# Tying a decode step's key products to the prompt's attention steps, and reordering the memory norm at the start

## The chip, the cores and the metric

One core of a Trainium2 chip runs the whole kernel. The metric is the device time of one execution in microseconds (us). A change of about 0.2% (4 us) is what a measurement of this kernel can tell from none.

## The reference

One layer of a decoder trunk is computed in fp32 for a prompt of 1024 tokens and for 8 decode rows with 2048 cached tokens each:

```python
xn = RMSNorm(x);  q, k, v, B, C, h, xq = split(xn @ w_in)
# branch A: stick-breaking attention, 8 heads x 64
z = q.k / 8 + b_sb[head]
log_keep = where(mask, log_sigmoid(-z), 0)
after = reverse_cumsum(log_keep) - log_keep
y_sb = where(mask, exp(log_sigmoid(z) + after), 0) @ v
# branch B: y_conv = B * causal_conv3(C * h)
# branch M: 4 heads, softmax attention into 256 memory tokens
mk, mv = split(RMSNorm(mem) @ w_mem_kv)
# merge by sigmoid gates of xn @ w_gate, project by w_o, add; then the squared-relu FFN, add
```

The decode rows take their past keys and values from pages of a pool (16 pages of 128 tokens for each row) and their memory keys from a cache. The outputs are also the new keys, values, conv states and the memory's keys and values.

## The kernel before

Every fp32 operand of a large matmul is split into a high part (a cast to fp32r on ScalarE) and a low part (the difference), and each product is three matmuls: high by high, high by low, low by high (`mm3`, L141 to L143). A weight block of 128 x 1024 comes by one DMA of 512 KB into one of two raw buffers (`weights`, L133); `split` casts it (L119) and subtracts (L120). The raw buffer is free for the next block when the subtraction is done. The subtraction runs on VectorE, but for the eight blocks of the memory's keys and values (`mk0` to `mk3`, `mv00` to `mv14`), whose blocks are given to GpSimd.

TensorE's order is written out by hand. A small planner (`Stream`) keeps a clock of its own: it walks a list of units (GEMMs of 10.3 us by its cost for the 1032 tokens), and between matmuls fires events that other generators asked for at a time of that clock: strips of the prompt's attention (`attention`), the memory attention (`xattn`), the decode rows (`decode`), and small transposes. TensorE executes in just this order. The order of the other engines and of the DMA queue is decided when the program is built, by a list scheduler with a timing model: it takes whatever is ready, the higher priority first. On the chip each engine then runs its own list strictly in order.

The parts that matter here:

- The start. The rows of the memory are loaded, squared and summed on ScalarE (L299), scaled (L300), put through Ln and Exp (L301, L302) and a Newton step (`newton`, L150 to L153), and multiplied (L305). TensorE transposes them (L314), ScalarE and VectorE make their high and low parts (L318, L319), and the memory's eight units begin. The prompt's rows go the same way, their transposes put between the memory's matmuls.
- The prompt's attention. A strip is 128 queries of two heads against up to eight key blocks; strips of five and more blocks are cut in two halves. Each head and half is one call of `zhalf`: four ScalarE steps, then on VectorE L639, L641, a scan (L642) and L648, with Ln and Exp on ScalarE. Eight strips make a pair of heads with 24 calls of `zhalf`, that is 96 of these VectorE steps; there are four pairs. The planner gives a pair 138.4 us (`ATT_NS`).
- The decode keys. For each row, eight tiles of two key pages (512 KB) come by DMA on SP (L835) into three buffers; VectorE multiplies a tile by the query (L928) and sums over each head (L929). With eight tiles of memory keys that is 72 such pairs of instructions ("products"), 4.2 us apart on the planner's clock (3.15 for the memory's). They and their loads have the lowest priority.

Of the kernel before, what the change touches and what calls it, by code (L numbers as in the profile page):

```python
# [12 lines left out]
AF = mybir.ActivationFunctionType  # L13
ALU = mybir.AluOpType
AX = mybir.AxisListType
# [3 lines left out]
P = 128  # L19
# [17 lines left out]
def body(ctx, tc, I, O):  # L37
    nc = tc.nc
# [10 lines left out]
    w_mkv = I["w_mem_kv"][0]  # L49
# [61 lines left out]
    stT = const.tile([P, 4, 16], F32, name="stT")  # L111
    ptab = const.tile([1, NB * NPG], I32, name="ptab")

    def tok_rows(p, s, t0, rows):
        return p[t0:t0 + rows] if t0 < S else s[t0 - S:t0 - S + rows]

    def split(hi, lo, src, scale=None, eng=None):
        if scale is None:
            nc.scalar.copy(out=hi, in_=src)  # L119
            (eng or nc.vector).tensor_tensor(out=lo, in0=src, in1=hi.bitcast(F32), op=ALU.subtract)  # L120
        else:
            nc.scalar.mul(out=hi, in_=src, mul=scale)
            nc.vector.scalar_tensor_tensor(out=lo, in0=src, scalar=scale, in1=hi.bitcast(F32),
                                           op0=ALU.mult, op1=ALU.subtract)
# [12 lines left out]
    def wview(w, c0, n, k0=0, k1=None):  # L137
        return w.rearrange("(k p) n -> p k n", p=P)[:, k0:k1, c0:c0 + n]
# [92 lines left out]
    def cost(n):  # L231
        return 3 * n / 2.4
# [19 lines left out]
    def high():  # L252
        return tc.high_priority(offset=HIGH)
# [38 lines left out]
    def norm_rows(tiles):  # L292
        junk = np_.tile([P, D], F32, name="junk", bufs=1)
        ss = np_.tile([P, 3, 3], F32, name="ss", bufs=4)
        v, r, t = (ss[:, i, :len(tiles)] for i in range(3))
        if tiles[-1][1] < P:
            nc.vector.memset(ss, 1.0)
        for i, (xt, rows) in enumerate(tiles):
            nc.scalar.activation(out=junk[:rows], in_=xt[:rows], func=AF.Square, accum_out=v[:rows, i:i + 1])  # L299
        nc.vector.tensor_scalar(out=v, in0=v, scalar1=1.0 / D, scalar2=EPS, op0=ALU.mult, op1=ALU.add)  # L300
        nc.scalar.activation(out=r, in_=v, func=AF.Ln)  # L301
        nc.scalar.activation(out=r, in_=r, func=AF.Exp, scale=-0.5)  # L302
        newton(r, v, t)
        for i, (xt, rows) in enumerate(tiles):
            nc.vector.tensor_scalar(out=xt[:rows], in0=xt[:rows], scalar1=r[:rows, i:i + 1], scalar2=None, op0=ALU.mult)  # L305

    def norm_col(tiles, gcol, dh, dl, k, pp=None, tag=None):
        n = sum(r for _, r in tiles)
# [13 lines left out]
    mem_rows = [load_rows(mem[t * P:t * P + P], P) for t in range(2)]  # L322
# [23 lines left out]
    def norm_mem():  # L346
        with high():
            first_vecs()
            norm_rows(mem_rows)
            for k in range(KT):  # L350
                norm_col(mem_rows, G_MEM, memh, meml, k)

# [30 lines left out]
    def mem_k(h):  # L383
        def body(wv, nxt):
            nxt()
            ps = pg.tile([P, 512], F32, name="g")[:, :NMEM]
            for k in range(KT):
                mm3(ps, wv[0][:, k], wv[1][:, k], memh[:, k], meml[:, k], k == 0, k == KT - 1)
                yield cost(NMEM)
            kf = np_.tile([P, NMEM], F32, name="mkf")  # L390
            nc.scalar.copy(out=kf, in_=ps)
            mk = np_.tile([P, 2, NMEM], F32R, name="mk")
            split(mk[:, 0], mk[:, 1], kf)
            nc.sync.dma_start(out=mkscr[h], in_=mk.bitcast(F32))

            @highp
            def late():
                pt = pf.tile([P, 4, P], F32, name="f")
                for t in range(2):
                    nc.tensor.transpose(out=pt[:, t], in_=kf[:, t * P:t * P + P], identity=ident)  # L400
                ko = np_.tile([P, 2, P], F32, name="mko")
                nc.vector.tensor_copy(out=ko, in_=pt[:, :2])
                nc.sync.dma_start(out=mk_prompt[:, h * P:(h + 1) * P].rearrange("(t p) d -> p t d", p=P), in_=ko)
            S_.at(1800, lambda: S_.when("f", late))
        return body
# [3 lines left out]
    def mem_v(hp, k0):  # L409
        def body(wv, nxt):  # L410
            nxt()
            if k0 == 0:
                mvps[hp] = [pg.tile([P, 512], F32, name="g")[:, :256] for t in range(2)]
            for k in range(4):
                for t in range(2):
                    ts = slice(t * P, t * P + P)
                    mm3(mvps[hp][t], memh[:, k0 + k, ts], meml[:, k0 + k, ts], wv[0][:, k], wv[1][:, k],
                        k0 + k == 0, k0 + k == KT - 1)
                    yield cost(256)
            if k0 == 0:  # L420
                return
            for t in range(2):
                vo = np_.tile([P, 256], F32, name="mvo")
                nc.scalar.copy(out=vo, in_=mvps[hp][t])
                nc.sync.dma_start(out=mv_prompt[t * P:t * P + P, hp * 256:hp * 256 + 256], in_=vo)
                mv = np_.tile([P, 2, 256], F32R, name="mv")
                split(mv[:, 0], mv[:, 1], vo)
                for i in range(2):
                    nc.sync.dma_start(out=mvscr[2 * hp:2 * hp + 2, :, i, t].rearrange("h p c -> p h c"),
                                      in_=mv[:, i].bitcast(F32).rearrange("p (h c) -> p h c", h=2))  # L430
        return body
# [120 lines left out]
    def add_gemm(name, src, body, eng=None):  # L552
        S_.add(name, lambda: weights(src, eng=eng), body)
# [73 lines left out]
    def zhalf(h, zt, qi, half, r):  # L627
        k0, k1 = halves(qi)[half]
        w_ = k1 - k0
        bias = bsb[:, h:h + 1]  # L630
        a = wk.tile([P, 512], F32, name="a", bufs=3)[:, :w_]
        u = wk.tile([P, 512], F32, name="u", bufs=2)[:, :w_]

        nc.scalar.activation(out=r, in_=zt[:, :w_], func=AF.Identity, bias=bias)
        nc.scalar.activation(out=a, in_=r, func=AF.Abs)
        nc.scalar.activation(out=a, in_=a, func=AF.Exp, scale=-1.0)
        nc.scalar.activation(out=u, in_=a, func=AF.Identity, bias=1.0)

        nc.vector.scalar_tensor_tensor(out=u, in0=u, scalar=-1.0, in1=a, op0=ALU.add, op1=ALU.subtract, reverse1=True)  # L639
        nc.scalar.activation(out=a, in_=a, func=AF.Ln, bias=1.0)  # L640
        nc.vector.tensor_tensor(out=u, in0=r, in1=u, op=ALU.max)  # L641
        nc.vector.tensor_tensor_scan(out=a[:, ::-1], data0=u[:, ::-1], data1=a[:, ::-1],  # L642
                                     initial=0.0 if half == 0 else carries.pop((h, qi)), op0=ALU.add, op1=ALU.add)
        if k0:
            carry = wk.tile([P, 1], F32, name="cy", bufs=6)
            nc.vector.tensor_copy(out=carry, in_=a[:, 0:1])
            carries[h, qi] = carry
        nc.vector.tensor_tensor(out=r, in0=r, in1=a, op=ALU.subtract)  # L648
        nc.scalar.activation(out=r, in_=r, func=AF.Exp)

    carries = {}

    ATT_NS = 138400.0
# [265 lines left out]
    def decode():  # L919
        yield "q3"  # L920
        yield 8000
        waiting = []

        def products(keep):
            while len(waiting) > keep:
                t, qb, out, d = waiting.pop(0)
                with low():
                    nc.vector.tensor_tensor(out=t, in0=t, in1=qb.unsqueeze(1).to_broadcast([P, 2, 512]), op=ALU.mult)  # L928
                    nc.vector.tensor_reduce(out=out, in_=t.rearrange("p g (h d) -> p g h d", d=d), axis=AX.X, op=ALU.add)  # L929

        def query(i, b):
            qb = dp.tile([P, 512], F32, name="qb", bufs=2)
# [3 lines left out]
        with low():  # L936
            qb = query(0, 0)
        for b in range(NB):
            for u in range(8):
                with low():  # L940
                    t = pages(kv_tile().rearrange("p (g c) -> p g c", g=2), k_pages, [b * NPG + 2 * u + j for j in range(2)])
# [6 lines left out]
            qb = nqb  # L948
        yield "x3p"
        for b in range(NB):  # L950
            with low():
                t = kv_tile().rearrange("p (t c) -> p t c", t=2)
# [7 lines left out]
        with low():  # L960
# [4 lines left out]
            for i in (1, 0):  # L965
                zh, m = zz[:, i * 512:(i + 1) * 512], wf[:, i * 512:(i + 1) * 512]
                a = dp.tile([P, 512], F32, name="da", bufs=2)
                d = dp.tile([P, 512], F32, name="dd", tag="va", bufs=3)
# [10 lines left out]
        for g0 in (12, 8, 4, 0):  # L979
            yield "f"  # L980
            pt = pf.tile([P, 4, P], F32, name="f")
            for g in range(4):
# [5 lines left out]
                                         initial=(0.0 if prev is None else prev[:, 0:1]), op0=ALU.add, op1=ALU.add)  # L988
# [37 lines left out]


    for h in range(4):
        add_gemm(f"mk{h}", wview(w_mkv, h * P, P), mem_k(h), nc.gpsimd)
    for hp in range(2):  # L1030
        for k0 in (0, 4):
            add_gemm(f"mv{hp}{k0}", wview(w_mkv, 512 + hp * 256, 256, k0, k0 + 4), mem_v(hp, k0), nc.gpsimd)
    S_._next()
    norm_mem()
    S_.spawn(norm_x())
    S_.run()
    p0.close()
# [417 lines left out]
```

## Time and profile before

| what | us |
|---|---|
| median of three runs | 1951.96 (1951.08 to 1953.09) |
| the profiled execution | 1949.08 |
| its span, first to last instruction | 1947.1 |
| TensorE busy | 1857.0 |
| VectorE busy | 1121.5 |
| ScalarE busy | 801.3 |
| GpSimd busy | 78.4 |

The profile is of one execution. PE is TensorE's matmuls, PEld its weight loads, DVE VectorE, ACT ScalarE, POOL GpSimd, SPq the queue of DMA issues on SyncE. A line such as L929 is that of the kernel's code. The span is 2 us shorter than the execution's time.

### The profile page before, as it was taken

The numbers are of one execution on the slowest core, as the hardware profiler recorded it, in microseconds if no ns is written. First come the engines' busy times: TensorE is split into PE (matmuls) and PEld (weight loads), VectorE is DVE, ScalarE is ACT, GpSimd is POOL, SyncE is SP. The second block draws the span as 40 slices with busy tenths as digits, with TensorE's granted clock in tenths as the row PEclk, the third lists the DMA queues.
The fourth block names the chain that finished last, engine by engine and source line by source line (L and its number), as shares of the span: only waits on it lengthen the run. The fifth ranks groups of instructions, "written<-read, shape, count | busy, mean of one in ns | idle before, by whom it ended". The sixth has DMA issues, their size and how long they took to land.

```text
span 1947.1 us, 31772 instructions
## 1 busy us (share of the span) xinstructions
PE 1857.0 (95%) x12226; PEld 1729.0 (89%) x12226; DVE 1121.5 (58%) x1899; ACT 801.3 (41%) x1641; POOL 78.4 (4%) x67
## 2 busy tenths in 40 slices
PE   5998797799999999999999999999999999999996
PEld 4987676698888777778999999999999999999996
DVE  5467999975647556541246547344555555554437
ACT  6323454567667666641334445522222111121223
POOL 3100000200000000000022000000000000000003
PEclk9999899899999999999999999999999999999998
DMA  7568777742322556675554523211111111111122
GB/s 241 163 206 257 227 227 242 236 124 90 97 82 93 175 176 207 196 236 188 172 182 142 158 81 110 66 44 55 44 55 49 50 44 44 44 44 46 53 88 88
DMA packets 219464, 249.14 MB, mean 128 GB/s; under 512 B 14488, under 2 KB 162672, under 8 KB 219312
## 3 DMA queue, kind: packets, MB, share of 16 engines
q1 hardware_dynamic: 204080, 230.17, 37.5%
q10 hardware_dynamic: 15008, 16.90, 2.5%
q8 instruction: 96, 1.57, 0.3%
q14 instruction: 56, 0.46, 0.1%
q0 software_dynamic: 224, 0.04, 0.0%
HBM read 201.67 MB, written 45.40 MB: 127 GB/s over the span
## 4 chain that ended last, share of the span: by engine, by line
PE 81%; DVE 10%; DMA 4%; issue 2%; ACT 2%; SPq 1%; DVEq 0%; ACTq 0%
PE g L141 9%; PE g L142 8%; PE g L143 8%; PE u L141 8%; PE u L142 8%; PE u L143 8%; PE w L141 6%; PE w L142 6%; PE w L143 6%; DMA kv<-in_cache_k_pages 2%; PE m L142 2%; PE m L141 2%; DVE kv L928 2%; PE m L143 2%; PE av L715 2%
## 5 line engine op out<-in xcount | busy, mean ns | idle before, releaser
L141 PE MATMUL g<-xh,wh 128*128 128x384 f32 (+1 forms) x1152 | 389.8, 338 | 4.1 <-DVE ql L120 4.0
L143 PE MATMUL g<-xh,wl 128*128 128x384 f32 (+1 forms) x1152 | 369.7, 321 | 1.9 <-DVE wl L120 1.9
L142 PE MATMUL g<-xl,wh 128*128 128x384 f32 (+1 forms) x1152 | 369.7, 321 | 0.0
L141 PEld LDWEIGHTS g<-xh,wh 128*128 128x128 f32 x1152 | 219.4, 190 | 41.7 <-issue 34.2
L1333 DVE TENSOR_TENSOR facc<-w,facc 128x384 f32<-128x384 f32 (+3 forms) x336 | 171.7, 515 | 141.7 <-PE w L143 141.7
L141 PE MATMUL w<-fh,dh 128*128 128x384 f32 (+3 forms) x720 | 231.5, 321 | 1.2 <-ACT facc L1331 1.0
L142 PE MATMUL w<-fl,dh 128*128 128x384 f32 (+3 forms) x720 | 230.4, 320 | 0.0
L143 PE MATMUL w<-fh,dl 128*128 128x384 f32 (+3 forms) x720 | 229.9, 319 | 0.0
L141 PE MATMUL u<-xh,wh 128*128 128x384 f32 (+1 forms) x720 | 229.3, 318 | 0.0
L143 PE MATMUL u<-xh,wl 128*128 128x384 f32 (+1 forms) x720 | 228.5, 317 | 0.0
L142 PE MATMUL u<-xl,wh 128*128 128x384 f32 (+1 forms) x720 | 228.4, 317 | 0.0
L143 PEld LDWEIGHTS g<-xh,wl 128*128 128x128 f32 x1152 | 218.9, 190 | 2.2 <-DVE wl L120 2.2
L142 PEld LDWEIGHTS g<-xl,wh 128*128 128x128 f32 x1152 | 219.9, 191 | 0.0
L120 DVE TENSOR_TENSOR wl<-wr,wh 128x1024 fp32r<-128x1024 f32 x96 | 117.7, 1227 | 108.9 <-ACT wh L119 108.9
L119 ACT CAST wh<-wr 128x1024 fp32r<-128x1024 f32 x104 | 109.0, 1048 | 96.9 <-PE g L142 47.5
L119 ACT CAST dh<-wr 128x1024 fp32r<-128x1024 f32 x32 | 33.5, 1050 | 256.2 <-PE w L142 239.6
L141 PEld LDWEIGHTS w<-fh,dh 128*128 128x128 f32 x720 | 135.6, 188 | 3.3 <-ACT facc L1331 1.2
L143 PEld LDWEIGHTS w<-fh,dl 128*128 128x128 f32 x720 | 135.7, 188 | 0.7
L142 PEld LDWEIGHTS w<-fl,dh 128*128 128x128 f32 x720 | 135.5, 188 | 0.6
L142 PEld LDWEIGHTS u<-xl,wh 128*128 128x128 f32 x720 | 135.4, 188 | 0.0
L141 PEld LDWEIGHTS u<-xh,wh 128*128 128x128 f32 x720 | 135.3, 188 | 0.0
L143 PEld LDWEIGHTS u<-xh,wl 128*128 128x128 f32 x720 | 135.1, 188 | 0.0
(292 smaller groups left out, 3439.8 us busy)
## 6 DMA issues: line engine op xcount, KB each, us to landing
kv<-in_cache_k_pages SPq DMA_DIRECT2D x128, 256.0 KB
kv<-in_cache_v_pages SPq DMA_DIRECT2D x96, 256.0 KB
wr<-in_w_up SPq DMA_DIRECT2D x32, 512.0 KB
wr<-in_w_down SPq DMA_DIRECT2D x32, 512.0 KB
wr<-in_w_in SPq DMA_DIRECT2D x28, 512.0 KB
lg<-lgscr SPq DMA_DIRECT2D x24, 516.0 KB
wr<-in_w_gate SPq DMA_DIRECT2D x24, 512.0 KB
lgscr<-lg ACTq DMA_DIRECT2D x48, 192.0 KB
```

What stands on the lines that cost most here:

```text
L119: nc.scalar.copy(out=hi, in_=src)
L120: (eng or nc.vector).tensor_tensor(out=lo, in0=src, in1=hi.bitcast(F32), op=ALU.subtract)
L141: nc.tensor.matmul(out=ps, lhsT=lh, rhs=rh, start=first, stop=False)
L142: nc.tensor.matmul(out=ps, lhsT=lh, rhs=rl, start=False, stop=False)
L143: nc.tensor.matmul(out=ps, lhsT=ll, rhs=rh, start=False, stop=last)
L715: nc.tensor.matmul(out=av[0][es], lhsT=hv[:, j, es], rhs=th[:, i, e], tile_position=(0, 64 * e), start=(r == R - 1 and i == 0), stop=(r == ...
L928: nc.vector.tensor_tensor(out=t, in0=t, in1=qb.unsqueeze(1).to_broadcast([P, 2, 512]), op=ALU.mult)
L1333: nc.vector.tensor_tensor(out=facc[:, n, cs], in0=ps, in1=facc[:, n, cs], op=ALU.add)
```

## The change

Three edits. First, the VectorE steps of `zhalf` are kept in a list, in the order in which the planner traces them. Each decode product gets an ordering edge: its multiplication comes no earlier in VectorE's list than step `at`, its sum no earlier than the step after it; `at` goes on by three with each product, but never beyond the last step traced so far. The edge is between instructions of one engine and adds no semaphore. Second, the memory norm is traced ahead of the first weights, and the first weight cast on ScalarE comes behind the norm's Exp. Third, the low parts of the memory's eight weight blocks are made on VectorE.

```diff
+    def behind(ins, first):
+        tc.add_manual_dep(ins.ins, first.ins.name, mybir.DependencyInfo(
+            mybir.DependencyClass.NoSync, mybir.DependencyReason.DATA), reason="behind")
+    first_exp = []
     def split(hi, lo, src, scale=None, eng=None):
         if scale is None:
-            nc.scalar.copy(out=hi, in_=src)
+            cast = nc.scalar.copy(out=hi, in_=src)
+            if first_exp:
+                behind(cast, first_exp.pop())
...
-        nc.scalar.activation(out=r, in_=r, func=AF.Exp, scale=-0.5)
+        ex = nc.scalar.activation(out=r, in_=r, func=AF.Exp, scale=-0.5)
...
+        return ex
...
-            norm_rows(mem_rows)
+            first_exp.append(norm_rows(mem_rows))
...
         (zhalf: L639, L641, L642 and L648 are each appended to steps)
...
-        waiting = []
+        waiting, at = [], [0]
...
-                    nc.vector.tensor_tensor(out=t, in0=t, in1=qb..., op=ALU.mult)
-                    nc.vector.tensor_reduce(out=out, in_=t..., axis=AX.X, op=ALU.add)
+                    p = nc.vector.tensor_tensor(out=t, in0=t, in1=qb..., op=ALU.mult)
+                    s = nc.vector.tensor_reduce(out=out, in_=t..., axis=AX.X, op=ALU.add)
+                    if steps:
+                        at[0] = min(at[0] + 3, len(steps) - 1)
+                        behind(p, steps[at[0]])
+                        behind(s, steps[min(at[0] + 1, len(steps) - 1)])
...
-        add_gemm(f"mk{h}", wview(w_mkv, h * P, P), mem_k(h), nc.gpsimd)
+        add_gemm(f"mk{h}", wview(w_mkv, h * P, P), mem_k(h))
...
-            add_gemm(f"mv{hp}{k0}", ..., mem_v(hp, k0), nc.gpsimd)
+            add_gemm(f"mv{hp}{k0}", ..., mem_v(hp, k0))
+    norm_mem()
     S_._next()
-    norm_mem()
```

## Rows read from the trace of the kernel before

**Rows 1.** The page's first part: busy us, share of the span, instructions.
```profile
PE 1857.0 (95%) x12226; PEld 1729.0 (89%) x12226; DVE 1121.5 (58%) x1899; ACT 801.3 (41%) x1641; POOL 78.4 (4%) x67
```
**Rows 2.** Windows by stage: us, busy us of each engine, granted clock, DMA.
```profile
0.00:64.00 64.00, 42.75 (x297) 38.15 (x298) 42.04 (x88) 41.40 (x84) 24.75 (x26) 1.00 0.73 230
64.00:110.00 46.00, 46.00 (x299) 45.65 (x298) 9.32 (x15) 11.34 (x20) 0.00 (x0) 1.00 0.45 141
110.00:386.00 276.00, 225.57 (x1497) 201.26 (x1496) 250.86 (x311) 122.84 (x276) 7.16 (x3) 0.91 0.76 236
386.00:543.00 157.00, 155.47 (x1070) 139.80 (x1069) 99.26 (x170) 104.75 (x231) 3.20 (x5) 1.00 0.34 107
```
**Rows 3.** The chain of waits, pieces from 360 to 369 us: start, us, what.
```profile
360.30 1.28 DVE a L642
361.58 0.50 DVE z L929
...
363.88 0.58 DVE pr L791
364.46 0.60 DVE m L648
365.06 1.14 DVE kv L928
```
**Rows 4.** TensorE's waits, 110 to 400 us: total us, times, longest.
```profile
PE f L797 <- DVE pr L791: 24.1, 3, 11.9
PE f L440 <- ACT qd L547: 8.1, 3, 3.1
```
**Rows 5.** VectorE's groups by shape, 100 to 400 us: busy us, mean ns.
```profile
L928 DVE TENSOR_TENSOR kv<-kv,qb 128x1024 f32<-128x1024 f32 x72 | 88.2, 1228 | 27.5 <-DMA kv<-in_cache_k_pages 20.6 <-DMA qb<-qscr 5.9 <-DMA kv<-in_cache_mem_k 1.0
L120 DVE TENSOR_TENSOR wl<-wr,wh 128x1024 fp32r<-128x1024 f32 x16 | 19.5, 1219 | 7.4 <-ACT wh L119 7.4
```
**Rows 6.** VectorE's timeline around the decode products and the pairs' first strips.
```profile
224.84 2.32 DVE L929 TENSOR_REDUCE z<-kv 128x16 f32<-128x1024 f32 x2
...
386.32 1.57 DVE L639 SCALAR_TENSOR_TENSOR u<-u,a 128x128 f32<-128x128 f32 x2
...
392.51 1.22 DVE L928 TENSOR_TENSOR kv<-kv,qb 128x1024 f32<-128x1024 f32 x1
...
542.97 0.29 DVE L639 SCALAR_TENSOR_TENSOR u<-u,a 128x128 f32<-128x128 f32 x1 [8.75 <-ACT u L637]
```
**Rows 7.** Windows, the stretch with the fullest VectorE, columns as above.
```profile
200.00:400.00 200.00, 161.19 (x1085) 142.85 (x1084) 193.82 (x250) 103.45 (x234) 10.16 (x5) 0.91 0.75 235
```
**Rows 8.** The DMA queue's waits on SP, 110 to 543 us.
```profile
SPq L133 <- DVE wl L120: 25.4, 9, 9.1
...
SPq L835 <- DVE z L929: 19.4, 21, 3.4
```
**Rows 9.** ScalarE and TensorE in the timeline of the start: start, us.
```profile
7.18 0.20 ACT L301 ACTIVATE ss<-ss 128x2 f32<-128x2 f32 x1 [0.24 <-DVE ss L300]
...
10.50 1.04 ACT L119 CAST wh<-wr 128x1024 fp32r<-128x1024 f32 x1 [3.12 <-DMA wr<-in_w_mem_kv]
11.45 0.20 ACT L302 ACTIVATE ss<-ss 128x2 f32<-128x2 f32 x1
...
15.43 0.48 PE L314 MATMUL z<-ident,xt 128*128 128x128 f32 x1 [9.29 <-DVE xt L305]
...
25.71 1.05 PE L314 MATMUL z<-ident,xt 128*128 128x128 f32 x2 [3.10 <-DVE xt L305]
```
**Rows 10.** GpSimd and VectorE in the timeline of the start.
```profile
11.63 2.34 POOL L120 TENSOR_TENSOR wl<-wr,wh 128x1024 fp32r<-128x1024 f32 x1 [5.89 <-ACT wh L119]
11.69 2.31 DVE L150 TENSOR_TENSOR ss<-ss 128x2 f32<-128x2 f32 x1 [4.54 <-ACT ss L302]
...
21.63 0.15 DVE L150 TENSOR_TENSOR ss<-ss 128x3 f32<-128x3 f32 x1
...
22.66 2.34 POOL L120 TENSOR_TENSOR wl<-wr,wh 128x1024 fp32r<-128x1024 f32 x1 [8.69 <-ACT wh L119]
22.68 4.20 DVE L305 TENSOR_SCALAR xt<-xt,ss 128x1024 f32<-128x1024 f32 x3
...
28.95 2.08 DVE L305 TENSOR_SCALAR xt<-xt,ss 128x1024 f32<-128x1024 f32 x3
```

More of the change, by code (lines that the diff above doesn't have):

```diff
@@ L637, in zhalf @@
         nc.scalar.activation(out=u, in_=a, func=AF.Identity, bias=1.0)
-        nc.vector.scalar_tensor_tensor(out=u, in0=u, scalar=-1.0, in1=a, op0=ALU.add, op1=ALU.subtract, reverse1=True)
+        steps.append(nc.vector.scalar_tensor_tensor(out=u, in0=u, scalar=-1.0, in1=a, op0=ALU.add, op1=ALU.subtract, reverse1=True))
         nc.scalar.activation(out=a, in_=a, func=AF.Ln, bias=1.0)
-        nc.vector.tensor_tensor(out=u, in0=r, in1=u, op=ALU.max)
-        nc.vector.tensor_tensor_scan(out=a[:, ::-1], data0=u[:, ::-1], data1=a[:, ::-1],
-                                     initial=0.0 if half == 0 else carries.pop((h, qi)), op0=ALU.add, op1=ALU.add)
+        steps.append(nc.vector.tensor_tensor(out=u, in0=r, in1=u, op=ALU.max))
+        steps.append(nc.vector.tensor_tensor_scan(out=a[:, ::-1], data0=u[:, ::-1], data1=a[:, ::-1],
+                                                  initial=0.0 if half == 0 else carries.pop((h, qi)), op0=ALU.add, op1=ALU.add))
         if k0:
@@ L647, in zhalf @@
             carries[h, qi] = carry
-        nc.vector.tensor_tensor(out=r, in0=r, in1=a, op=ALU.subtract)
+        steps.append(nc.vector.tensor_tensor(out=r, in0=r, in1=a, op=ALU.subtract))
         nc.scalar.activation(out=r, in_=r, func=AF.Exp)
+    steps = []
     carries = {}
@@ L927, in products @@
                 with low():
-                    nc.vector.tensor_tensor(out=t, in0=t, in1=qb.unsqueeze(1).to_broadcast([P, 2, 512]), op=ALU.mult)
-                    nc.vector.tensor_reduce(out=out, in_=t.rearrange("p g (h d) -> p g h d", d=d), axis=AX.X, op=ALU.add)
+                    p = nc.vector.tensor_tensor(out=t, in0=t, in1=qb.unsqueeze(1).to_broadcast([P, 2, 512]), op=ALU.mult)
+                    s = nc.vector.tensor_reduce(out=out, in_=t.rearrange("p g (h d) -> p g h d", d=d), axis=AX.X, op=ALU.add)
+                    if steps:
+                        at[0] = min(at[0] + 3, len(steps) - 1)
+                        behind(p, steps[at[0]])
+                        behind(s, steps[min(at[0] + 1, len(steps) - 1)])
         def query(i, b):
@@ L1028, in body @@
     for h in range(4):
-        add_gemm(f"mk{h}", wview(w_mkv, h * P, P), mem_k(h), nc.gpsimd)
+        add_gemm(f"mk{h}", wview(w_mkv, h * P, P), mem_k(h))
     for hp in range(2):
         for k0 in (0, 4):
-            add_gemm(f"mv{hp}{k0}", wview(w_mkv, 512 + hp * 256, 256, k0, k0 + 4), mem_v(hp, k0), nc.gpsimd)
+            add_gemm(f"mv{hp}{k0}", wview(w_mkv, 512 + hp * 256, 256, k0, k0 + 4), mem_v(hp, k0))
+    norm_mem()
     S_._next()
-    norm_mem()
     S_.spawn(norm_x())
```

## The prediction

> **What bounds the kernel now.** I read the page's busy times first: TensorE is busy 1857 of 1947.1 us and nothing else comes near [rows 1]. So only about 90 us of idle TensorE, and whatever it ran at the lower clock, can be won at all. Next the windows by stage [rows 2]. From 64 to 110 us TensorE is full and a step moved there costs or gives nothing of itself. Two stretches are not full: the start, where TensorE is busy 42.8 of 64 us, and 110 to 386 us, where it is busy 225.6 of 276 us at a mean granted clock of 0.91 (a mix of the 2.4 and 1.2 GHz levels; in the other stages it stands at 1.00). In that second stretch VectorE is busy 250.9 of 276 us, and 193.8 of the 200 us from 200 to 400 [rows 7]. Just behind it, 386 to 543, VectorE has 99.3 us of work in 157 and TensorE is full. The reader is to see a load put in the wrong place: VectorE overflows in one stage and has 58 us to spare in the next.
>
> The chain of waits says the same piece by piece [rows 3]: a decode product, a scan, a decode sum, a softmax step, a strip's last step, a product, all on VectorE, one behind the other. TensorE's longest waits there are for such a queued step: 24.1 us in three for the memory attention's division, and 8.1 in three for a copy that ScalarE makes late because VectorE holds it up [rows 4].
>
> **How the decode keys lie, before and after.** All 72 multiplications lie ahead of 400 us [rows 5], and the last but one or two run when the second pair of heads begins: its first strip is at 386.3, the last multiplication at 392.5 [rows 6]. So 70 of 72 products share the first pair's stage.
>
> For the order after, I follow the planner's clock from the constants in the code. q3's GEMM ends at its time 41.3, the first strip is traced near 60, the second pair's first near 217, the third pair's near 361. A product comes every 4.2 us plus what the events in between add (about 4.4); `at` goes on by three and is cut to the last traced step at the first strip and at the end of a pair. That ties products 3 to 37 to the 96 steps of the first pair, 38 to 71 to the second pair's, and the 72nd to the third pair's first strip. Thirty-three products move from the first pair's stage into the second's. TensorE's order does not change, since the tied instructions add nothing to the planner's clock.
>
> **The terms.** Two sums back to back take 2.32 us, a multiplication 1.23 alone and about as much as a sum in a row [rows 5, 6], so a product is 2.32 us of VectorE. Thirty-three are 76.6 us. VectorE in 110 to 386 goes from 250.9 to 174.3, in 386 to 543 from 99.3 to 175.9; together 350.2 as before.
>
> What TensorE needs: the second pair took 542.97 - 386.32 = 156.7 us with TensorE full, for 144 us of the planner, a factor of 1.09. The first stretch is 217 - 41.3 = 175.7 us of planner time, so 191.5 us, where it takes 276: 84.5 lost. A second way to it, 225.6 us busy x 0.91 = 205 at full clock, gives 71 lost. So together TensorE needs 348 to 362 us, VectorE 350, and the two stages take 433.
>
> Both engines would then be full at once, and neither can be. VectorE cannot be filled ahead of the strips: some 48 us (planner 41 to 85) hold seven products and an estimated half as much other work, 24 us. The other 326 us of VectorE's work run in a queue like today's. If the queue is as tight as from 200 to 400 (193.8/200 = 0.97 [rows 7]) that is 336 us and the stages take 384, a gain of 49; if it is as loose as the whole stretch (250.9/276 = 0.91 [rows 2], which holds 27.5 us of waits for pages and queries [rows 5]) it is 358 and 406, a gain of 27. I take 38, near the middle. The outer bounds: a queue without any gap, 48 + 326 = 374, gains 59; a queue at 0.85 (326/0.85 = 384) gives the whole back, 0.
>
> What hides the moved work is VectorE's 58 us of idle time in the second pair; it doesn't hide all, for 175.9 is 19 us more than that stage's 157, so TensorE's waits come back there, shorter. That is in the sum already.
>
> **The norm ahead of the cast.** Ln ends at 7.38 and Exp starts at 11.45, behind a cast that itself waits for its weights until 10.50 [rows 9]. Exp comes right behind Ln in the new order, so up to 4.1 us earlier. What is late next is VectorE's Newton step, below. The cast isn't made later: its weights land at 10.5 anyway.
>
> **No low parts on GpSimd.** Eight subtractions of 2.34 us on GpSimd become eight of 1.22 on VectorE [rows 5, 10], 9.8 us more on VectorE. But the first Newton step took 2.31 us beside GpSimd's subtraction and the same step 0.15 alone, and three row scalings took 4.20 beside one and 2.08 alone [rows 10]: 2.2 and 2.1 us that TensorE waited through, as its first transposes waited until 15.43 and the prompt's until 25.71 [rows 9]. So VectorE pays about two us or so at each meeting already; over eight subtractions the 9.8 us are about what it pays now. The Trainium skill, SBUF — State Buffer, section Who interferes with whom, states that a VectorE instruction with two SBUF inputs, or in a two-port mode, and a GpSimd instruction that reads SBUF block each other for a whole instruction; by that rule, and the trace agrees, every meeting goes. [...]
>
> Upper bound of the start: 4.1 + 2.2 + 2.1 = 8.4 us. Lower bound 0: the prompt's rows or the second weight block land no earlier (their DMAs share a queue at 0.73 of its engines [rows 2]), and TensorE is full from 28 us on. I take 5, nearer the upper end, because both waits are ones for VectorE. All of it passes through to the end, as 64 to 110 is TensorE's own time.
>
> **The sum.** 38 + 5 = 43. The profiled execution took 1949.1 us (span 1947.1): 1906. The runs' median is 1952.0, 2.9 above it: 1909. A measurement tells about 0.2%, 4 us, from no change.
>
> **The rivals.**
>
> *Slower: page loads stall the DMA queue.* SP runs in order, and a page load waits for the sum three products earlier. Today that is 19.4 us in 21 waits, 3.4 at most, while weight loads have waited for their raw buffer up to 9.1 us and cost nothing [rows 8]. Tied sums come later and on another engine's pace; a weight load behind such a wait comes late, and TensorE with it. The two stages have some 28 units; if each lost 3 us to it, 84 us would go against the 43: 1993. It decides from 43/28 = 1.5 us for each. For it: nothing paces SP to the new order. Against it: three buffers and a unit's lead, and TensorE's waits of today name VectorE, not a load. 7 in 100.
>
> *The stall only moves.* The second pair's VectorE is over its window by 19 us, and where the queue there is looser than 0.91 (strips that wait for ScalarE between steps, products in order behind them), the gain shrinks to 5 to 20 us: near 1939. For it: each pair's last strips hold 13 products' ties in a row with the shortest window behind them. 15 in 100.
>
> *No change.* The list scheduler might already have placed products behind such steps, or the waits might be refilled by something else. Against it: 70 products by 386 us cannot stay there under the ties. 5 in 100, at 1950.
>
> *More.* VectorE's queue has no gaps and the clock stays up: 59 + 8 = 67, so 1885. 11 in 100.
>
> **How the numbers follow.** The forecast has 62 in 100, its own range a gain of 27 to 57, so 1895 to 1925. The range of 8 in 10 takes in the larger gain and most of the moved stall: 1882 to 1942. Faster by over 0.2% are the forecast, the larger gain and the moved stall, 0.88; within 0.2% is 0.05; slower is 0.07.
>
> **What would show it.** The second pair's first strip near 345 us instead of 386, with some 37 products ahead of it; VectorE busy 0.8 to 0.95 from there to the third pair's first strip, which comes near 500 instead of 543; the division's waits (24.1 us) mostly gone, and the granted clock of the first stretch above 0.95. Exp at about 7.5, the first Newton step at 0.15, first transposes near 9.5, q3's end near 105. Wrong would make it: products that still crowd into the first pair, page loads late in the second, or waits for weights on TensorE.

## The result, and the profile after

The changed kernel takes 1932.2 us (median of 4 runs, 1931.9 to 1933.8) where the kernel before took 1952.5 in the runs beside it. The ratio is 0.9898, with a 95% interval of 0.9881 to 0.9916. It is faster by 20.3 us, a little under half of the 43 forecast; the time is within the range. The profiled execution took 1931.9 us with a span of 1930.1, 17.0 less than the span before.

The page's first part again, to be read against [rows 1]: GpSimd has 17 us less to do, and TensorE is still the one full engine.

```profile
PE 1851.1 (96%) x12226; PEld 1726.4 (89%) x12226; DVE 1120.2 (58%) x1907; ACT 800.1 (41%) x1641; POOL 61.6 (3%) x59
```

The windows by stage of the kernel after, cut at its own stages, stand against [rows 2]; the last row is the first pair's stage without its first 50 us.

```profile
0.00:64.00 64.00, 44.55 (x312) 40.10 (x313) 41.99 (x99) 42.92 (x87) 5.25 (x18) 1.00 0.77 242
108.00:334.00 226.00, 207.40 (x1457) 187.88 (x1456) 175.36 (x244) 115.37 (x265) 0.00 (x0) 0.98 0.66 204
334.00:529.00 195.00, 171.95 (x1142) 154.09 (x1140) 175.80 (x237) 112.73 (x245) 13.05 (x7) 0.93 0.59 182
529.00:684.00 155.00, 154.04 (x1073) 129.55 (x1073) 97.91 (x175) 105.20 (x240) 0.10 (x1) 1.00 0.43 134
158.00:334.00 176.00, 159.23 (x1104) 141.38 (x1105) 151.04 (x212) 103.25 (x234) 0.00 (x0) 0.98 0.66 204
```

The reader is to see the forecast loads (174.3 and 175.9 us of VectorE; they are 175.36 and 175.80), a first stage near full clock, and a second pair that is now the bad one: 195 us, of which TensorE is busy 172 at a mean granted clock of 0.93. Here is where the 17.0 us of span come from, in us; a stage ends with the first strip of the next pair, and q3's end is its last evacuation.

| kernel | q3's end | to the second pair | second pair | the two together |
|---|---|---|---|---|
| before | 110.1 | 276.2 | 156.7 | 432.8 |
| after | 108.3 | 225.7 | 194.6 | 420.3 |

So in these two profiles 1.8 came from the start, 50.5 from the first pair's stage, 38.0 were given back in the second pair, and 2.6 more came in the third.

TensorE's waits of the kernel after between 108 and 529 us (columns as in [rows 4]) have the same line on top as before, and 17.2 of its 25.8 us lie in the second pair:

```profile
PE f L808 <- DVE pr L802: 25.8, 5, 10.7
PE wt L709 <- ACT m L659: 4.9, 4, 2.7
PE f L450 <- ACT qd L557: 3.5, 3, 1.9
```

The longest of these waits, in the timeline of the kernel after (VectorE's instructions in order of time, then the one of TensorE that waited, then GpSimd's, and last a division that runs at another time):

```profile
487.51 0.67 DVE L796 TENSOR_REDUCE mx<-f 128x2 f32<-128x512 f32 x1
488.11 2.82 DVE L652 TENSOR_TENSOR_SCAN a<-u,a 128x512 f32<-128x512 f32 x1
490.85 1.19 DVE L939 TENSOR_TENSOR kv<-kv,qb 128x1024 f32<-128x1024 f32 x1
491.96 1.21 DVE L652 TENSOR_TENSOR_SCAN a<-u,a 128x512 f32<-128x512 f32 x1
493.10 1.19 DVE L940 TENSOR_REDUCE xs<-kv 128x8 f32<-128x1024 f32 x1
494.21 0.15 DVE L797 TENSOR_SCALAR mx<-mx 128x2 f32<-128x2 f32 x1
...
498.40 0.15 DVE L801 RECIPROCAL sm<-sm 128x2 f32<-128x2 f32 x1
498.47 1.68 DVE L649 SCALAR_TENSOR_TENSOR u<-u,a 128x512 f32<-128x512 f32 x1
500.07 2.29 DVE L939 TENSOR_TENSOR kv<-kv,qb 128x1024 f32<-128x1024 f32 x1
502.28 1.75 DVE L802 TENSOR_TENSOR pr<-pr,sm 128x512 f32<-128x512 f32 x1
...
504.17 1.08 PE L808 MATMUL f<-ident,pr 128*128 128x128 f32 x4 [10.70 <-DVE pr L802]
...
484.19 5.65 POOL L978 TENSOR_TENSOR z<-z,bsb 128x1024 f32<-128x1024 f32 x1 [3.78 <-DVE z L940]
...
497.95 3.32 POOL L990 TENSOR_TENSOR w<-w,dd 128x512 f32<-128x512 f32 x2 [8.11 <-DVE dd L989]
501.24 3.91 POOL L992 TENSOR_TENSOR w<-w,da 128x512 f32<-128x512 f32 x2
...
426.11 0.67 DVE L802 TENSOR_TENSOR pr<-pr,sm 128x512 f32<-128x512 f32 x1
```

The memory attention's softmax needs five short steps: a maximum (L796), its scaling (L797), the Exp on ScalarE, a reciprocal (L801) and the division (L802). On VectorE the four that are its own take 0.67 + 0.15 + 0.15 + 1.75 = 2.7 us here. From the maximum's start to the division's end it is 16.5, because at every step products, scans and strip steps stand ahead of them in VectorE's list. A part of the 16.5 us is GpSimd's: beside its steps a scan takes 2.82 us, a strip step (L649) 1.68, a product 2.29 and the division 1.75, where the same shapes take 1.21, 0.67, 1.2 and 0.67 elsewhere in this execution, some 4.8 us more together. That holds for this wait alone. The next longest, 6.5 and 6.4 us, have no instruction of GpSimd near them; there the five steps take 12.2 and 12.9 us. The order of the work puts 7.7 us of planner time between scores and transposes; TensorE had run out of it at 493.5. It executes its list in order, so it stood for 10.7 us. Its granted clock in that place, in windows of the same execution:

```profile
480.00:490.00 10.00, 10.00 (x63) 8.57 (x62) 10.00 (x12) 4.71 (x9) 5.75 (x2) 1.00 0.74 233
490.00:500.00 10.00, 3.47 (x25) 2.78 (x24) 10.00 (x15) 10.00 (x22) 2.05 (x2) 0.88 0.64 212
500.00:505.00 5.00, 0.83 (x5) 0.86 (x5) 5.00 (x4) 1.82 (x4) 5.00 (x3) 0.50 0.23 49
505.00:510.00 5.00, 5.00 (x30) 5.00 (x29) 5.00 (x7) 1.22 (x2) 0.15 (x1) 0.71 0.29 109
510.00:515.00 5.00, 5.00 (x35) 4.54 (x35) 5.00 (x7) 2.16 (x3) 0.00 (x0) 1.00 0.32 65
```

VectorE is full in all five windows. TensorE stands from 493.5 to 504.2, the granted clock falls to the lower of its two levels (0.50 is 1.2 GHz), and from 505 to 510, when TensorE is busy throughout, it is 0.71 on average.

The DMA queue's waits on SP in the kernel after, 108 to 529 us, against [rows 8]: the wait for the sum three products earlier has tripled, but TensorE's waits of that stretch name no load.

```profile
SPq L846 <- DVE z L940: 59.4, 32, 7.3
...
SPq L142 <- DVE wl L129: 10.9, 12, 2.7
```

The start after, in the timeline, against [rows 9, 10]:

```profile
7.29 0.21 ACT L311 ACTIVATE ss<-ss 128x2 f32<-128x2 f32 x1
7.52 0.16 DVE L159 TENSOR_TENSOR ss<-ss 128x2 f32<-128x2 f32 x1 [0.51 <-ACT ss L311]
9.13 0.48 PE L324 MATMUL z<-ident,xt 128*128 128x128 f32 x1 [2.74 <-DVE xt L314]
11.06 1.04 ACT L126 CAST wh<-wr 128x1024 fp32r<-128x1024 f32 x1 [3.57 <-DMA wr<-in_w_mem_kv]
12.57 1.06 ACT L308 ACTIVATE junk<-xt 128x1024 f32<-128x1024 f32 x1 [0.47 <-DMA xt<-in_x_prompt]
14.38 1.06 ACT L308 ACTIVATE junk<-xt 128x1024 f32<-128x1024 f32 x1 [0.66 <-DMA xt<-in_x_prompt]
15.44 0.46 ACT L328 ACTIVATE memh<-z,vecs 128x256 fp32r<-128x256 f32 x1
...
16.46 0.69 PE L324 MATMUL z<-ident,xt 128*128 128x128 f32 x2 [4.92 <-DVE meml L329]
23.98 2.07 DVE L314 TENSOR_SCALAR xt<-xt,ss 128x1024 f32<-128x1024 f32 x3
24.88 1.05 PE L324 MATMUL z<-ident,xt 128*128 128x128 f32 x2 [3.64 <-DVE xt L314]
```

Exp, Newton step and first transposes come as forecast (start at 7.29, 0.16 long, start at 9.13). But ScalarE works its list in order, and in it the cast and two of the prompt's squares, each waiting for its own DMA, now stand ahead of the memory's first high part (15.44). The low part comes behind it, and TensorE, which had won 6.3 us at its first transposes, stops for 4.92 at the fifth pair of them. The prompt's transposes start 0.8 us earlier than before.

### The profile page after: what moved, and what is told of

Read it like the earlier page. It is cut to its first block, busy times and chain, and to the rows that moved or that the text cites. A ratio compares the mean times of both kernels' runs of the same rounds, so it can differ in the third digit from the quotient of the medians.

```text
span 1930.1 us, 31777 instructions
## 1 busy us (share of the span) xinstructions
PE 1851.1 (96%) x12226; PEld 1726.4 (89%) x12226; DVE 1120.2 (58%) x1907; ACT 800.1 (41%) x1641; POOL 61.6 (3%) x59
## 4 chain that ended last, share of the span: by engine, by line
PE 81%; DVE 10%; DMA 3%; ACT 3%; issue 3%; SPq 0%; DVEq 0%; ACTq 0%
PE g L150 9%; PE g L152 8%; PE g L151 8%; PE u L150 8%; PE u L151 8%; PE u L152 8%; PE w L150 6%; PE w L151 6%; PE w L152 6%; PE m L151 2%; PE m L150 2%; PE m L152 2%; PE f L888 2%; DVE kv L939 2%; PE av L726 2%
## 5 line engine op out<-in xcount | busy, mean ns | idle before, releaser
L129 DVE TENSOR_TENSOR wl<-wr,wh 128x1024 fp32r<-128x1024 f32 x104 | 127.4, 1225 | 115.0 <-ACT wh L126 114.8
```

## The experiments

Two theories of the missing half were to be told apart. By the first, the moved work fits, but products lengthen the line in front of the memory softmax's short steps, and TensorE's order gives that chain too little cover. By the second, VectorE is simply over its capacity in the second pair (176 us of work in 157), whoever TensorE is seen to wait for. Diffs are against the changed kernel unless another is named; ratios are to the kernel before, run beside, with 95% intervals; stages are those of the table above.

**The ties alone** (`e1_ties`): memory norm and GpSimd's low parts as before.

```diff
-        add_gemm(f"mk{h}", wview(w_mkv, h * P, P), mem_k(h))
+        add_gemm(f"mk{h}", wview(w_mkv, h * P, P), mem_k(h), nc.gpsimd)
...
-    norm_mem()
     S_._next()
+    norm_mem()
```

> The ties alone, with the start of the kernel before. Theory A (the gain is that of the ties, first pair of heads 50 us shorter, second pair 38 us longer; the start's edits give 2 us): 1933 to 1936, ratio 0.990 to 0.992, third pair's first strip some 12 to 15 us earlier than in the kernel before. Rival B (the ties gain next to nothing net, the rest is the start's): above 1944.

Measured: 1936.3 us, 0.9918 (0.9905 to 0.9932). Stages 223.1 and 193.3, together 416.5. The ties are 16 us of the gain, and they alone make the pattern of the table, the wait of 10.7 us included.

**The norm ahead alone** (`e2_norm`: `if steps:` becomes `if False:`, low parts on GpSimd) and **low parts on VectorE alone** (`e3_lo`: the kernel before without `, nc.gpsimd`).

> The norm ahead of the first weights alone, low parts still on GpSimd, no ties. Theory A (the wait moves from the Exp to the memory's high parts, which ScalarE runs behind the cast and the prompt's squares): first transposes near 9 us instead of 15.4, but the first matmuls of the memory's first unit no more than 1 us earlier than 20.3, q3's last evacuation near 109.5 instead of 110.1; time within 2 us of the kernel before. Rival B (the early transposes carry through): q3's last evacuation near 105, 5 us off the time.

> The low parts on VectorE alone, the old order of the norm, no ties. Theory A (GpSimd's subtractions cost VectorE as much by blocking as they take off it): the Newton step near 0.15 us and three row scalings near 2.1, q3's last evacuation 1 to 2 us earlier than 110.1; time 0 to 2 us less. Rival B (VectorE is the limit of the start, and 9.8 us of subtractions more slow it): q3's last evacuation later than 110.1, by up to 9 us.

Measured: 1953.3 us, 1.0001 (0.9990 to 1.0013), and 1953.4, 1.0009 (1.0000 to 1.0018). Neither gains anything by itself. With the norm alone the first transposes come at 9.44, and TensorE then waits 3.57 us at 15.42 for a low part. With the low parts alone q3 ends at 106.7, 3.5 us earlier than before, and the second pair begins at 387.1, 0.8 later. That what TensorE wins by q3's end is lost again in a stage that VectorE bounds is one reading; it isn't shown, as q3's end differs by 3 us between two profiles of the same start (last section).

**Both edits of the start, without the ties** (`e11_start`):

```diff
-                    if steps:
+                    if False:
```

> Both edits of the start, no ties. Theory A (the start gains 2 to 4 us by q3's end, and where VectorE is the limit of the next stage, as it is without the ties, that is lost again): q3's last evacuation 106 to 109, the second pair's first strip at 384 to 388, time within 3 us of the kernel before. Rival B (the start's gain passes through to the end without the ties too): 1946 to 1949.

Measured: 1948.8 us, 0.9983 (0.9975 to 0.9992), about 3.4 us. So by the times the two pay only together, though this interval just touches that of `e2_norm`, and they add to the ties: 0.9918 x 0.9983 = 0.9901, against 0.9898 measured for the whole change. As rival B had it, the gain passes through the stage that VectorE bounds. The profile, of an execution of 1950.7 us, doesn't show where it arises: q3's end is at 109.1 and the second pair at 386.7. Why the low parts alone gain nothing wasn't settled.

**ScalarE's list at the start** (`e7_sq`): the prompt's first squares go behind the memory's last high part.

```diff
+            if late is not None:
+                behind(sq, late)
...
-        norm_rows(tiles)
+        norm_rows(tiles, last_high[0])
```

> The whole change, and the squares of the prompt's first rows come on ScalarE behind the last of the memory's high parts. Theory A (the start's gain went to ScalarE's list: the cast and two squares ahead of the memory's high parts held them to 15.4 us): the high parts begin by 12.5, the wait of 4.9 us for the low parts goes, the prompt's first transposes come 1 to 4 us earlier than 24.9, q3's last evacuation near 106 instead of 108.3; time 1 to 4 us less than 1932. Rival B (the prompt's rows or the second weight block set the start): q3's last evacuation within 1 us of 108.3.

Measured: 1932.8 us, 0.9900 (0.9883 to 0.9918), no different from the whole change. Two rows of TensorE's timeline in this kernel:

```profile
14.15 0.69 PE L326 MATMUL z<-ident,xt 128*128 128x128 f32 x2 [2.16 <-DVE meml L331]
...
25.51 1.05 PE L326 MATMUL z<-ident,xt 128*128 128x128 f32 x2 [7.47 <-DVE xt L316]
```

The wait for low parts shrinks from 4.92 to 2.16 us, and the wait for the prompt's rows grows from 3.64 to 7.47. Theory A's early high parts come (12.35 us), its gain doesn't. But the edit itself sends the prompt's first square from 12.57 to 16.53 us, and with it the prompt's own chain of squares and norm. What the start would be with both chains early isn't shown.

**Ties two steps apart instead of three** (`e4_two`): some 50 products stay in the first pair, some 21 go to the second.

```diff
-                        at[0] = min(at[0] + 3, len(steps) - 1)
+                        at[0] = min(at[0] + 2, len(steps) - 1)
```

> The whole change, but the tie goes on by two steps for each product instead of three, so 48 products are tied to the first pair's 96 steps and 24 to the second's (now 37 and 35). Theory A (each pair's stage has a limit of its own, and the second is over its VectorE capacity by 19 us): the first pair's stage grows from 226 us to 235 to 245, the second's shrinks from 195 to 165 to 180; the sum 400 to 420 against 420, the time 1912 to 1932. Rival B (only the total of VectorE's work counts, wherever it lies): the sum stays at 418 to 423. Rival C (the first pair pays more than the second gets): above 1936.

Measured: 1945.7 us, 0.9971 (0.9961 to 0.9980), so rival C came true: the first pair pays more than the second gets. The windows of its two stages:

```profile
108.00:356.00 248.00, 211.47 (x1452) 189.96 (x1452) 205.42 (x271) 116.17 (x263) 0.00 (x0) 0.94 0.71 219
356.00:539.00 183.00, 168.17 (x1115) 151.02 (x1114) 144.12 (x209) 111.73 (x246) 8.64 (x7) 0.95 0.48 151
```

In its second pair VectorE has 144 us of work, less than the 157 of a full TensorE, so by capacity that stage should be whole again. It takes 182.4 us, 25.7 over, with VectorE busy 0.79 of it. The theory of capacity alone falls. The division's wait is there in both stages, 19.8 and 8.9 us; in the second pair 5.9 us of waits for a strip's last step come on top.

**Half of each product** (`e6_half`): the second page of each tile is left out, so half of the decode scores stay zero; all loads are made.

```diff
-                    p = nc.vector.tensor_tensor(out=t, in0=t, in1=qb.unsqueeze(1).to_broadcast([P, 2, 512]), op=ALU.mult)
+                    p = nc.vector.tensor_tensor(out=t[:, 0:1], in0=t[:, 0:1], in1=qb.unsqueeze(1), op=ALU.mult)
...
     (the sum is cut to t[:, 0:1] in the same way)
```

> The whole change, but each product multiplies and sums only the first of its tile's two pages, so that it takes about 1.2 us of VectorE instead of 2.3, and half of the decode scores are left zero; the page loads are all made. Theory A (each product in VectorE's list passes about half of its length on to TensorE): the second pair's stage from 195 to 172 to 180, the first's from 226 to 208 to 218, the time 1898 to 1912. Rival B (only the excess over VectorE's capacity counts, and none is left): the second pair's stage 157 to 164. Rival C (the order, the loads or the queue cost it, not VectorE's time): both stages as they are, the time above 1925.

Measured: 1898.8 us, 0.9720 (0.9704 to 0.9736); stages 215.0 and 169.6. In TensorE's waits no division is left. With as many instructions in nearly the same places, each shorter, the chain fits under its cover. Since the load falls too, by some 80 us over the two stages, this run doesn't tell the two theories apart by itself.

**More cover for the chain** (`e8_cover`): of the memory attention's three gaps in planner time the middle one, between scores and transposes, grows from 7.7 to 13.3 us, the other two shrink to 4.9, so their sum stays 23.1. VectorE's instructions stay the same.

```diff
                 yield "f"
                 sc = pf.tile([P, 2, 256], F32, name="f")
...
-                yield XA_NS
+                yield 13300.0
                 yield "f"
                 pt = pf.tile([P, 2, 256], F32, name="f")
```

> The whole change, and of the planner's three gaps of 7.7 us in each round of the memory attention the one between its scores and its transposes is 13.3 us, the other two 4.9, so that a round is as long as before. Theory A (what is left of the loss is TensorE's wait for the memory softmax's division, 8.6 us in the first pair and 17.2 in the second, and the lower clock behind it): these waits fall below 5 us together, the first pair's stage to 210 to 218 us, the second's from 195 to 168 to 178, the time to 1895 to 1912. Rival B (VectorE's list is too full, so TensorE waits for other steps in its place): the second pair's stage stays above 188, the time within 5 us of 1932. Rival C (the gaps that were cut bring new waits, for the queries' load or for the split of the weights): above 1936.

Measured: 1914.9 us (1911.9 to 1916.1), 0.9802 (0.9787 to 0.9816): 17 us below the whole change, and 3 above what theory A allowed. Its windows and its waits from 109 to 508 us:

```profile
109.00:328.00 219.00, 204.56 (x1443) 185.15 (x1443) 174.27 (x243) 114.40 (x263) 0.00 (x0) 0.98 0.69 207
328.00:508.00 180.00, 167.54 (x1131) 149.91 (x1130) 164.83 (x230) 112.79 (x249) 19.40 (x7) 0.98 0.61 188
```

```profile
PE f L450 <- ACT qd L557: 9.1, 4, 3.1
PE wt L709 <- ACT m L659: 6.0, 4, 3.8
PE f L151 <- DVE xtl L129: 3.9, 2, 2.7
PE f L150 <- ACT xth L126: 3.2, 1, 3.2
...
PE f L808 <- DVE pr L802: 1.2, 1, 1.2
```

The division's wait goes from 25.8 to 1.2 us, the granted clock of the second pair from 0.93 to 0.98, and the two stages from 420.3 to 399.5. The five steps still take 11 to 12 us at six of the nine places that begin by 470 us; now they are covered. At the ninth, where they took 16.5 us, they take 11.1, and no step of them is drawn out beside GpSimd. In the second pair 7.1 us of waits are new, for the parts behind one of the gaps that were cut (xtl, xth). One thing moved besides: 32 products instead of 35 lie in the second pair and 3 in the third. In the first pair, where 37 lie in both kernels, the stage is 6.4 us shorter; of the second pair's 14.4 a part may be due to those 3, though in `e4_two` that stage took 182.4 us with only 21.

**The same cover without the ties** (`e9_bcover`: the three gaps in the kernel before).

> The kernel before with the same gaps as the run above, no ties and no edits of the start. Theory A (the division's waits, 24.1 us, are a part of the first pair's loss, but VectorE is full there at 0.91 to 0.97, so most of them come back at other steps): the first pair's stage from 276 to 262 to 276, the time 1938 to 1952. Rival B (the division alone is what TensorE waits for, ties or not): the stage near 245, the time near 1920.

Measured: 1955.3 us, 1.0011 (1.0002 to 1.0020). Its first stage, the window ahead of the second pair and the one behind, and its longest wait behind 113 us:

```profile
113.00:368.00 255.00, 219.21 (x1470) 195.05 (x1469) 232.31 (x294) 116.43 (x265) 0.00 (x0) 0.94 0.77 233
368.00:548.00 180.00, 160.62 (x1085) 144.31 (x1084) 123.18 (x191) 111.45 (x245) 9.60 (x7) 0.95 0.40 126
```

```profile
PE wt L698 <- ACT m L649: 21.8, 5, 16.0
```

The division's wait is nearly gone here too (2.0 us), and the first stage 20 us shorter, but 9 products spill into the second pair untied and TensorE stands there for a strip's last step for 16.0 us. Neither theory's time came true. Cover alone gives nothing, the ties alone 16 us, both together with the start's edits 38.

**Other gaps** (`e10_gaps`: 6.5, 13.3 and 6.5 us; the decode queries' transposes 6.5 us late instead of 2.5).

> The run with the longer gap ahead of the memory attention's transposes, and now the two gaps that it had cut are 6.5 us instead of 4.9, and the small transposes of the memory queries' decode rows come 6.5 us after their GEMM instead of 2.5. Theory A (what is left are waits of TensorE in order, each for a step that is late by less than a gap: 9.1 us for the rows' copy in the first pair, 7.1 for the split of the memory's weights in the second): both waits below 3 us, the first pair's stage from 219 to 208 to 214, the second's from 180 to 170 to 176, the time 1898 to 1908 against 1915. Rival B (VectorE's list is what is full, and the waits go on to the strips' steps): within 4 us of 1915.

Measured: 1917.9 us, 0.9825 (0.9808 to 0.9842). The waits of `e8_cover` for xtl, xth and qd shrink, others take their place (5.4 us for a weight's low part, 7.2 for a strip's last step): no gain over it, as rival B had it.

**The decode softmax's GpSimd steps on VectorE** (`e12_zdve`: `e8_cover`, with the steps of L978, L990 and L992 on VectorE).

> The run with the longer gap, and the five steps that GpSimd does for the decode softmax run on VectorE (some 4 us there). Theory A (those five steps hold VectorE's instructions with two inputs for about as long as they run, in the second pair's stage): no VectorE step there longer than its usual time, the stage from 180 to 174 to 179, the time 1908 to 1914. Rival B (they cost VectorE nothing that TensorE waits for): within 2 us of 1915, or later by up to 4.

Measured: 1910.1 us (1908.0 to 1916.3), 0.9783 (0.9770 to 0.9796), the fastest version, 42 us under the kernel before. Its interval still touches that of `e8_cover`, so its own part, some 4 us, isn't certain. Its second pair, and a scan there, of 128x512 like the one of 2.82 us above:

```profile
328.00:505.00 177.00, 168.99 (x1132) 151.73 (x1131) 162.92 (x231) 112.30 (x243) 0.20 (x2) 0.96 0.62 192
```

```profile
495.12 1.27 DVE L652 TENSOR_TENSOR_SCAN a<-u,cy,a 128x512 f32<-128x512 f32 x1
```

VectorE took over GpSimd's steps (19.40 us there) and still has 2 us less to do in that stage than in `e8_cover`. One product fewer lies in it, which is 2.3 us; over the whole kernel VectorE is busy 1115.7 us with five instructions more, against 1115.8, so taking them over cost it nothing. GpSimd's steps on VectorE without the longer cover, where they stood beside the 10.7 us wait, weren't run.

## Why the prediction was half right

**The order after: right.** 37 products lie ahead of the second pair's first strip, as counted from the planner's clock, and all 72 ahead of the third's, where the last was forecast at that strip. The loads of VectorE came within 1 us, and behind the first 50 us of the stage it has 151.0 + 175.8 = 326.8 us of work where 326 were forecast.

**What TensorE needs: the higher bound was right.** In the first stage 207.4 us x 0.98 = 203 at full clock, against 205 and 191.5; the estimate by the planner's factor was too low there.

**"The other 326 us of VectorE's work run in a queue like today's": this step failed.** It assumed a queue at 0.91 to 0.97 of VectorE's time, 347 us at the middle; it took 371 (158 to 529 us), 0.88. Those 24 us are nearly the whole 25 by which the two stages missed their 395. In the first pair it ran at 0.86 (151 of 176 us), in the second at 0.90. The largest of VectorE's 44 us of gaps in that stretch (columns as in [rows 4]):

```profile
DVE u L649 <- ACT u L647: 17.2, 8, 4.0
DVE mx L796 <- PE f L152: 9.0, 2, 8.5
```

So VectorE came to wait for a strip's steps on ScalarE and for scores from TensorE. The prediction took the tight queue of [rows 7] for a property of the load. In the kernel before, 70 products lie there untied; that they kept the queue so tight is argued, not tested. TensorE paid for it with the division's wait in that very stage. The sum also ran both stages as one queue of VectorE, but in the first pair VectorE was no longer the limit: it had 175 us of work where TensorE needed 203.

The forecast that the 24.1 us of [rows 4] would mostly go had no working behind it: it treated them as an effect of too much load in the stage, but they come from the number of instructions ahead of four short steps against 7.7 us of cover. The ties change the load and leave such a line in front. When TensorE stands, scores and strips come later, and VectorE then has gaps as well. That this wait sets most of the price, the runs show: longer cover takes it from 25.8 to 1.2 us and some 17 us off the kernel with the same VectorE instructions (`e8_cover`, where VectorE's gaps for scores fall to 0.7 us and those for strips stay at 18.0), shorter products remove it (`e6_half`, which lowers the load too), and a second pair with VectorE at 0.79 is 25.7 us over all the same (`e4_two`). Of the 6 us that are left of the missing 23 some 2 are the start's (below); the others stay open.

**The rival "the stall only moves" came nearest:** it gave a gain of 5 to 20 us and a time near 1939. Its mechanism had the place, the second pair, and the looser queue right, but put the stall at the strips' steps. VectorE's own gaps for such steps are 17.2 us, most of them in the first pair; of the second pair's 23 us of idle TensorE 17.2 are the division's. The rest of what that stage is over is the lower clock: 195 us against 172 x 0.93 = 160 at full clock.

**The slower rival fell.** SP's waits for sums did grow, from 19.4 to 59.4 us and 7.3 at most, and cost nothing that TensorE's waits show.

**The start: mechanism right, size too large.** Forecast 5, measured 3.4 by times (`e11_start`) and 1.8 in this one profile. The 2.2 and 2.1 us of blocking went as forecast (Newton step 0.16, three scalings 2.07). The Trainium skill, SBUF — State Buffer, section Who interferes with whom, has that rule, and the trace agrees once more: a scan of the same shape takes 2.82 us beside GpSimd's addition and 1.21 alone. What the term lacked is the next instruction in ScalarE's list: the high parts stand behind a cast and squares that wait for DMAs. The lower bound had named the prompt's rows; `e7_sq` moves the wait to them, but by holding their squares back, so what sets the start behind the high parts stays open.

**Still open:** `e12_zdve` leaves the second pair at 177 us, 20 over a full TensorE. The waits there are short ones, for a strip's last step and for the memory attention's parts; `e10_gaps` moved them and didn't lower them.

## What to carry to other kernels

Moving load off a full engine is half of the work: list the short steps of that engine which TensorE waits for in order, and compare the cover in TensorE's order with the instructions that can stand ahead of them, even where the engine is only 0.8 busy. Spreading the filler and lengthening the cover paid 16 us and nothing alone, and together, with some 3 us from the start, 38. Where a wait at a start is removed, read the next entries of every in-order list, with the DMAs that they wait for, before counting the gain.

## What the runs showed of the hardware

A stop of TensorE costs more than its length: the granted clock is 0.50 from 500 to 505 us, at the end of the 10.7 us wait, and 0.71 from 505 to 510, when TensorE is busy again. VectorE and GpSimd hold each other up: in the same place a division takes 1.75 us instead of 0.67 and a product 2.29 instead of 1.2, and GpSimd's addition takes 5.65 where it took 2.39 in the kernel before. The start of one and the same code also varies: q3's end came at 110.1 us before and at 113.2 with the ties alone, whose start is the same; the mean granted clock of the first 64 us was 1.00 in the one execution and 0.97 in the other. So a start's gain of 3 us can't be read from two profiles, only from the times of several runs; the 1.8 us of the table is no more than that.
